# Seven half-products for eight in 24 of the 32 w_up tiles, with w_down's products between them

## The chip, the cores and the metric

The kernel runs on one NeuronCore of a Trainium2 chip, as one launch. The metric is device time in microseconds (us), the median of several runs; smaller is better. The engines are TensorE (PE in the profile; PEld is its weight load), VectorE (DVE), ScalarE (ACT), GpSimd (POOL) and SyncE (SP), which starts most DMAs. Each engine works through its own instructions in order and waits for others by semaphores.

## What is computed

A two-layer decoder trunk over 512 tokens of width 1024, in float32: two kinds of attention, gated and added, an output projection, then an MLP. The MLP is where the change lies:

```python
    x = x + mixed @ w_out
    h = rmsnorm(x, norm_mlp)
    return x + jnp.square(jax.nn.relu(h @ w_up)) @ w_down
```

`w_up` is 1024 x 4096, `w_down` 4096 x 1024. A final rmsnorm follows the second layer.

## The kernel before

Everything is kept transposed: features on the 128 partitions, the 512 tokens along the free axis. x is eight tiles of 128 x 512. A product with a weight matrix makes output tiles of 128 columns of the weight, each from eight K tiles.

Each float32 operand is split into two float32r parts, a high one (`h`, a rounding copy made on ACT) and a low one (`lo`, what is left, made by a subtraction on DVE or POOL). `gemm` (L202) makes three matmuls per K tile: high by high, high by low, low by high. So an output tile of w_up or w_down is 8 x 3 = 24 matmuls of 128 x 128 by 128 x 512.

Weights come in a fixed order, the list that `order` (L678) yields. `fetch` (L161) starts the next 512 KB load into a `raw` buffer on SP's queue; `convert` (L169) splits the oldest loaded one, `wh` by a cast on ACT (L182) and `wl` by a subtraction on DVE (L183), and fetches again; `weights` (L187) hands out the split parts. `gemm` calls `ahead` after its second K tile, so that the next weights are split while this product runs. There are two `raw`, two `wh` and two `wl` buffers.

A list scheduler puts the instructions of each engine in an order when the program is built, from the order of the source and its own costs; the order in the source is therefore not always the order on an engine. Buffers of one tag are a pool (`BUFS`, L150): an allocation waits until one of them is free.

The MLP of a layer (L902 to L945) goes in four chunks of 1024 columns of w_up. A chunk is eight up tiles, each 24 matmuls into one of PSUM's eight banks (`bank`, in turn), and then eight down tiles, each 24 matmuls over the chunk's eight activations, added to x on DVE (L939). The norm's factor per token, R, comes out of `rstd` (L256) while the first up tiles run; the input `u` is x times the gain only, and `act` (L906) applies R afterwards:

```python
            nc.vector.scalar_tensor_tensor(t, ps, 0.0, R, op0=OP.max, op1=OP.mult)   # L908
            nc.scalar.activation(h, t, AF.Square)                                    # L911
            nc.gpsimd.tensor_tensor(t, t, t, op=OP.mult)                             # L912
            nc.gpsimd.tensor_tensor(lo, t, h.bitcast(F32), op=OP.subtract)           # L913
```

The last chunk's down tiles of the second layer are `last` (L949), which works on 256 tokens at a time, so its matmuls have 256 columns, and ends with the final norm and the output. `sumsq` (L234) adds up squares on POOL (L249); `make_u` (L226) makes `u`.

Of the kernel before, what the change touches and what calls it, by code (L numbers as in the profile page):

```python
# [11 lines left out]
F32 = mybir.dt.float32  # L12
F32R = mybir.dt.float32r
# [4 lines left out]
L = 2  # L18
# [56 lines left out]
def col_blocks(w):  # L75
    """[K, M] -> [M/128, 128 (row in K tile), K/128, 128 (column)]"""
    k, m = w.shape
    return np.ascontiguousarray(w.reshape(k // 128, 128, m // 128, 128).transpose(2, 1, 0, 3))


def row_chunks(w):
    """[1024, M] -> [4, 128, 2, M]: two K tiles a chunk"""
    return np.ascontiguousarray(w.reshape(4, 2, 128, w.shape[1]).transpose(0, 2, 1, 3))


def layout(a):
    d = {}
    d["xT"] = np.ascontiguousarray(a["x"].reshape(T, D).T.reshape(KT, 128, T))
    wb, wva, wg2, wo, wout, wup, wdn, w1, small = ([] for _ in range(9))
    for l in range(L):  # L90
# [19 lines left out]
        wdn.append(np.stack([col_blocks(a["w_down"][l][c * 1024:(c + 1) * 1024]) for c in range(4)]))  # L110
# [14 lines left out]
    d["wout"], d["wup"], d["wdn"], d["w1"], d["small"] = st(wout), st(wup), st(wdn), st(w1), st(small)  # L125
# [15 lines left out]
class Body:  # L141
# [27 lines left out]
    def convert(self):  # L169
        """Splits the next loaded weights into two float32r parts, and starts a load in their place."""  # L170
# [16 lines left out]
    def weights(self, src, n=1024):  # L187
        """The parts of src, which is the next of the plan."""
# [35 lines left out]
    # ---- norms  # L224
# [9 lines left out]
    def sumsq(self, x, acc, last=False):  # L234
        """adds x * x to the list of tiles whose sum over tiles and partitions is wanted"""
# [51 lines left out]
    # ---- projections in token layout  # L287
# [30 lines left out]
    # ---- pairs of heads  # L318
# [37 lines left out]
    def q_pair(self, x, fox=False):  # L356
        """[q hi; q lo] of both heads, and with `fox` [q hi; 1; 1; 0 ...] of each."""
# [17 lines left out]
    # ---- causal attention of one head  # L375
# [73 lines left out]
    def out_half(self, O, o, e):  # L449
        """o[64e:64e+64] = O[:64] + O[64:]"""  # L450
# [124 lines left out]
    def cmp_probs(self, hk, q2):  # L575
        """Probabilities of the four heads of kv head hk over the compressed blocks, transposed."""
# [41 lines left out]
    # ---- a layer  # L618
# [16 lines left out]
    def forget(self, z):  # L635
        """cumulative log sigmoid, negated: CC rows 0-7 its upper part, rows 32-39 the rest"""
# [27 lines left out]
    def bank(self):  # L664
        """a bank of PSUM, any of the eight in turn"""
# [8 lines left out]
    def order(self, l):  # L674
        """The weights of a layer in the order of their use: [name, source, columns]"""
# [22 lines left out]
        for c in range(4):  # L698
            yield from ((flat(a["wup"][l, 8 * c + j]), 1024) for j in range(8))
            yield from ((flat(a["wdn"][l, c, m]), 1024) for m in range(8))  # L700

    def layer(self, l, u):
        nc, a = self.nc, self.a
        wb = a["wb"][l].rearrange("m p k c -> m p (k c)")
        # values of FoX and NSA, forget and branch gates: tokens on partitions
# [52 lines left out]
        # FoX  # L758
# [39 lines left out]
        # NSA  # L798
# [26 lines left out]
        def half(kind, m, w):  # L825
            """y_a or y_b, output tile m"""
# [39 lines left out]
        # gates of NSA, the mix, output projection  # L866
# [35 lines left out]
        # MLP  # L902
        R = None
        pend = []

# [10 lines left out]
        for c in range(4):  # L916
# [170 lines left out]
```

## Time and profile before

| | |
|---|---|
| median of 3 runs | 1568.53 us (1568.13 to 1568.83) |
| span of the profiled execution | 1567.0 us |
| MLP of the first layer, about | 430 to 780 us of the span |
| MLP of the second layer, about | 1205 us to the end |
| HBM read | 140.77 MB |

The span runs from the first to the last instruction of one profiled execution; the median is over other executions, without a profile, and is 1.5 us longer. In a row of a timeline stand the start, the duration, engine, line, operation, the tile written and the tiles read, their sizes, and in brackets how long the engine had been idle and what released it. In a row of groups stand the count, busy time, mean duration in ns, and idle time before. In a row of one tile or line: the shortest, median and longest duration in ns. In a row of windows: the length of the window, the busy time of PE, PEld, DVE, ACT and POOL with counts, the granted PE clock (1.00 is full), the busy share of the DMA engines and GB/s. A row of waits tells which engine and line waited for which, the total, how often, and the longest.

### The profile page before, as it was taken

How to read it: one execution, taken by the hardware profiler on the slowest of the kernel's cores; microseconds unless marked ns; L12 is line 12 of the kernel's file. 1: busy time of each engine (PE TensorE's matmuls, PEld its weight loads, DVE VectorE, ACT ScalarE, POOL GpSimd, SP SyncE). 2: the span in 40 equal slices, each digit the busy share in tenths (PEclk: the TensorE clock that was granted, in tenths of full speed). 3: DMA queues.
4: the chain of work that ended last, by engine and by line, in shares of the span. 5: the costliest groups of instructions: out<-in, count | busy, mean ns of one | idle time of the engine just before them, and what ended most of it. 6: DMA issues, size and time to landing. Idle time of an engine off the chain costs nothing.

```text
span 1567.0 us, 20175 instructions
## 1 busy us (share of the span) xinstructions
PE 1553.8 (99%) x7596; PEld 1282.8 (82%) x7596; DVE 885.4 (57%) x1804; ACT 627.3 (40%) x1135; POOL 258.5 (16%) x209
## 2 busy tenths in 40 slices
PE   9999999999999999999999999999999999999997
PEld 8867888888888888888887688888888888888887
DVE  5687988866443333333646689887564433333343
ACT  6444665543432222223443456555434312222243
POOL 4000000000241322304400000000002504132252
PEclk9999999999999999999999999999999999999999
DMA  6545422132222222222435543222322222232231
GB/s 238 169 133 156 118 81 81 61 108 97 98 94 95 94 101 101 95 95 101 177 115 166 160 132 95 68 68 68 120 96 94 95 94 95 99 103 95 95 121 54
DMA packets 56625, 169.42 MB, mean 108 GB/s; under 512 B 7344, under 2 KB 8112, under 8 KB 56528
## 3 DMA queue, kind: packets, MB, share of 16 engines
q1 hardware_dynamic: 53072, 161.84, 32.2%
q10 hardware_dynamic: 3456, 6.29, 1.2%
q8 instruction: 60, 0.98, 0.2%
q14 instruction: 37, 0.30, 0.1%
HBM read 140.77 MB, written 4.19 MB: 93 GB/s over the span
## 4 chain that ended last, share of the span: by engine, by line
PE 77%; issue 13%; POOL 6%; DVE 3%; ACT 1%; DMA 0%; POOLq 0%; DVEq 0%; SPq 0%; ACTq 0%
PE ps_mm L208 12%; PE ps_mm L209 11%; PE ps_mm L210 11%; PE ps_O L443 4%; PE ps_PT L417 3%; POOL tmp L912 3%; PE ps_S L208 3%; PE ps_S L210 3%; PE ps_S L209 3%; PE ps_PT L208 3%; POOL ol L913 3%; PE ps_PT L210 3%; PE ps_PT L209 3%; PE ps_O L210 3%; PE ps_O L209 2%
## 5 line engine op out<-in xcount | busy, mean ns | idle before, releaser
L182 ACT CAST wh<-raw 128x1024 fp32r<-128x1024 f32 (+2 forms) x235 | 243.3, 1036 | 612.4 <-PE ps_mm L209 155.9
L183 DVE TENSOR_TENSOR wl<-raw,wh 128x1024 fp32r<-128x1024 f32 (+2 forms) x235 | 287.1, 1222 | 53.6 <-ACT wh L182 45.1
L208 PE MATMUL ps_mm<-uh,wh 128*128 128x512 f32 x608 | 242.8, 399 | 0.0
L210 PE MATMUL ps_mm<-uh,wl 128*128 128x512 f32 x608 | 239.9, 395 | 0.0
L209 PE MATMUL ps_mm<-ul,wh 128*128 128x512 f32 x608 | 239.8, 394 | 0.0
L912 POOL TENSOR_TENSOR tmp<-tmp 128x512 f32<-128x512 f32 x64 | 97.5, 1524 | 440.5 <-ACT oh L911 440.5
L395 ACT ACTIVATE E<-E,mx 128x128 f32<-128x128 f32 x192 | 108.0, 563 | 81.6 <-DVE mx L394 74.5
L208 PEld LDWEIGHTS ps_mm<-uh,wh 128*128 128x128 f32 x608 | 114.3, 188 | 30.3 <-issue 10.6
L210 PEld LDWEIGHTS ps_mm<-uh,wl 128*128 128x128 f32 x608 | 114.3, 188 | 24.0 <-issue 0.8
L209 PEld LDWEIGHTS ps_mm<-ul,wh 128*128 128x128 f32 x608 | 114.6, 189 | 18.8
L209 PE MATMUL ps_mm<-ol,wh 128*128 128x512 f32 (+1 forms) x288 | 111.4, 387 | 0.6 <-POOL ol L913 0.6
L208 PE MATMUL ps_mm<-oh,wh 128*128 128x512 f32 (+1 forms) x288 | 111.7, 388 | 0.0
L210 PE MATMUL ps_mm<-oh,wl 128*128 128x512 f32 (+1 forms) x288 | 111.4, 387 | 0.0
L426 ACT CAST pth<-ps_PT 128x512 fp32r<-128x512 f32 x144 | 72.8, 512 | 94.9 <-PE ps_PT L417 94.7
L394 DVE CUSTOM_DVE_ANT_0 E<-ps_S,ct 128x128 f32<-128x128 f32 x192 | 92.3, 484 | 26.6 <-PE ps_S L391 25.2
L249 POOL TENSOR_TENSOR acc<-sq 128x512 f32<-128x512 f32 (+1 forms) x6 | 8.4, 1405 | 594.5 <-DVE wl L183 580.5
L427 DVE TENSOR_TENSOR ptl<-ps_PT,pth 128x512 fp32r<-128x512 f32 x144 | 85.1, 596 | 27.7 <-ACT pth L426 27.3
L417 PE MATMUL ps_PT<-ct,E 128*128 128x128 f32 x480 | 83.1, 274 | 1.4 <-DVE ptl L427 1.4
L913 POOL TENSOR_TENSOR ol<-tmp,oh 128x512 fp32r<-128x512 f32 x64 | 83.3, 1301 | 5.0
L417 PEld LDWEIGHTS ps_PT<-ct,E 128*128 128x128 f32 x480 | 60.1, 140 | 14.7 <-DVE ptl L427 4.2
L388 PE MATMUL ps_S<-kd,q 128*128 128x256 f32 x192 | 63.8, 338 | 0.0
L208 PEld LDWEIGHTS ps_mm<-oh,wh 128*128 128x128 f32 x288 | 54.2, 188 | 11.0 <-issue 1.5
(325 smaller groups left out, 3223.7 us busy)
## 6 DMA issues: line engine op xcount, KB each, us to landing
raw<-wb SPq DMA_DIRECT2D x64, 512.0 KB, 3.5
raw<-wup SPq DMA_DIRECT2D x64, 512.0 KB, 3.5
raw<-wdn SPq DMA_DIRECT2D x64, 512.0 KB, 3.4
kd<-hl SPq DMA_DIRECT2D x48, 256.0 KB, 4.7
w<-w SPq DMA_DIRECT2D x32, 256.0 KB, 5.9
q<-hl SPq DMA_DIRECT2D x64, 128.0 KB, 3.2
raw<-wo SPq DMA_DIRECT2D x16, 512.0 KB, 3.5
raw<-wout SPq DMA_DIRECT2D x16, 512.0 KB, 3.4
```

Source lines behind the costliest of these rows:

```text
L182: nc.scalar.copy(h[:, :n], raw[:, :n])
L183: nc.vector.tensor_tensor(lo[:, :n], raw[:, :n], h[:, :n].bitcast(F32), op=OP.subtract)
L208: mm(ps, h[:, c], xh, start=start and i == 0, stop=False)
L209: mm(ps, h[:, c], xl, start=False, stop=False)
L210: mm(ps, lo[:, c], xh, start=False, stop=stop and i == ks - 1)
L394: nc.vector.tensor_tensor_reduce(e, ps[:, :n], self.mask[:, T - n:], -1.0, BIG, OP.add, OP.min, mx)
L395: nc.scalar.activation(e, e, AF.Exp, bias=mx, scale=-1.0, accum_out=sm[:, i:i + 1])
L417: nc.tensor.transpose(ps[:, j * 128:(j + 1) * 128], E[i][:, b * 128:(b + 1) * 128], self.ident)
L426: nc.scalar.copy(h[:, o:o + n], ps[:, :n])
L427: nc.vector.tensor_sub(lo[:, o:o + n], ps[:, :n], h[:, o:o + n].bitcast(F32))
L912: nc.gpsimd.tensor_tensor(t, t, t, op=OP.mult)
L913: nc.gpsimd.tensor_tensor(lo, t, h.bitcast(F32), op=OP.subtract)
```

## The change

The first eight up tiles of a layer (`PLAIN`) stay as they were. The other 24 are made in twelve pairs by Strassen's scheme in Winograd's form. A pair's weights (1024 rows, 256 columns) are cut into four quarters A11, A12, A21, A22 of 512 rows by 128 columns, the normalised input into four quarters B of 512 rows by 256 tokens. Seven products of such quarters and of their sums and differences, each 4 K tiles x 3 matmuls of 128 x 128 by 128 x 256, give the four quarters of the two output tiles, where the plain way has eight such products.

`prepare` makes the seven input operands once per layer, split into high and low parts: it needs R applied first. Its steps are taken between the plain tiles, four a tile, and during the first six down blocks. `Strassen.load` fetches the raw weights of a pair (two loads of 512 KB) two pairs ahead, `Strassen.convert` makes the seven weight operands of the next pair (two sums on POOL, two on DVE, seven high parts on ACT, seven low parts on DVE) while `unit` makes the products of this one. The outputs come out of seven combinations on DVE and one copy on ACT, and `Strassen.act` applies relu, square and the split (three operations on ACT, one on POOL).

The down products of the first six groups of 512 rows of w_down (`wd2`) are made in 48 blocks of 4 x 3 matmuls, each added to x: six after the plain tiles, then four between the products of each pair (two in the eleventh pair, none in the twelfth). One 512 KB load holds the weights of two blocks; its raw buffer is the single one of the tag `crs`. The last 1024 rows stay as eight down tiles (or `last`).

In the built program the new steps of `prepare` stand on DVE among the evacuations of the plain tiles and the splits of their weights; after R, in the first layer, two evacuations, the first round of `prepare` with the third evacuation in it, then the split of the fifth plain tile's weights, and so on; the order is the same in the second layer.

Line numbers in the diff's new parts, where the text names them, are those of the changed kernel. Comments and docstrings that the diff only strikes out are left out here.

```diff
@@ layout
-        wdn.append(np.stack([col_blocks(a["w_down"][l][c * 1024:(c + 1) * 1024]) for c in range(4)]))
+        wdn.append(col_blocks(a["w_down"][l][3072:]))
+        b = a["w_down"][l][:3072].reshape(6, 4, 128, 4, 2, 128)
+        wd2.append(b.transpose(0, 3, 2, 4, 1, 5).reshape(6, 4, 128, 1024))
@@ fetch
-            src, n = self.plan.popleft()
-            raw = self.t(self.raws.popleft() if self.raws else "raw", [128, 1024], name="raw")
+            src, n, *tag = self.plan.popleft()
+            tag = tag[0] if tag else self.raws.popleft() if self.raws else "raw"
+            raw = self.t(tag, [128, 1024], name="raw")
@@ order
-        for c in range(4):
-            yield from ((flat(a["wup"][l, 8 * c + j]), 1024) for j in range(8))
-            yield from ((flat(a["wdn"][l, c, m]), 1024) for m in range(8))
+        yield from ((flat(a["wup"][l, j]), 1024) for j in range(self.PLAIN))
+        yield from ((a["wd2"][l, c, m], 1024, "crs") for c in range(6) for m in range(4))
+        yield from ((flat(a["wdn"][l, m]), 1024, *(("crs",) if m == 0 else ())) for m in range(8))
@@ the MLP, now mlp
+        def down(c, m, w):
+            ps = self.bank()
+            yield from self.gemm(ps, w, 4 * (m % 2), acts[4 * c:4 * c + 4], ks=4)
+            nc.vector.tensor_add(x[m], x[m], ps)
...
+        S = Strassen(self, l, x, gm)
+        D = downs()
+        g0 = self.PLAIN // 2
+        S.load(g0)
+        for j in range(self.PLAIN):
+            ps = self.bank()
+            w = self.weights(a["wup"][l, j].rearrange("p k c -> p (k c)"))
+            run(self.gemm(ps, w, 0, u))
...
+                R, _ = self.rstd(acc, (self.turn_tag(), self.turn_tag()))
+                prep = S.prepare(R)
...
+            act(ps)
+            for _ in range(4):
+                next(prep, None)
+        S.load(g0 + 1)
+        conv = S.convert(g0)
+        for i in range(6):
+            next(D)()
+            next(prep, None)
+            next(prep, None)
+            if i == 3:
+                run(prep)
+            if i > 3:
+                for _ in range(2):
+                    next(conv, None)
+        run(conv)
+        for g in range(g0, 16):
+            S.load(g + 2)
+            n = 4 if g < 14 else 2 if g == 14 else 0
+            S.unit(g, D, n, acts)
@@ new: class Strassen
+    def prepare(self, R):
...
+        for p in range(4):
+            q = []
+            for i in (p, p + 4):
+                t = b.t("t2", [128, T], name="bs")
+                V.scalar_tensor_tensor(t, self.x[i], self.gm[:, i:i + 1], R, op0=OP.mult, op1=OP.mult)
+                q.append(t)
+                yield
+            (b11, b12), (b21, b22) = ((t[:, :256], t[:, 256:]) for t in q)
+            t12, t34 = (b.t("t2", [128, 2, 256], name="ts") for _ in range(2))
+            V.tensor_tensor(t12[:, 0], b12, b11, op=OP.subtract)
+            V.tensor_tensor(t12[:, 1], b22, t12[:, 0], op=OP.subtract)
+            yield
+            V.tensor_tensor(t34[:, 0], b12, b22, op=OP.subtract)
+            V.tensor_tensor(t34[:, 1], b21, t12[:, 1], op=OP.subtract)
+            yield
+            A = nc.scalar
+            A.copy(t12h[:, :, p], t12)
+            A.copy(t34h[:, :, p], t34)
+            A.copy(h11[:, p], b11)
+            A.copy(h21[:, p], b21)
+            A.activation(h22[:, p], b22, AF.Copy, scale=-1.0)
+            f = lambda ap: ap.bitcast(F32)
+            V.tensor_tensor(t12l[:, :, p], t12, f(t12h[:, :, p]), op=OP.subtract)
+            yield
+            V.tensor_tensor(t3l[:, p], t34[:, 0], f(t34h[:, 0, p]), op=OP.subtract)
+            V.tensor_tensor(t4l[:, p], t34[:, 1], f(t34h[:, 1, p]), op=OP.subtract)
+            yield
+            V.tensor_tensor(l11[:, p], b11, f(h11[:, p]), op=OP.subtract)
+            V.tensor_tensor(l21[:, p], b21, f(h21[:, p]), op=OP.subtract)
+            yield
+            V.scalar_tensor_tensor(l22[:, p], b22, -1.0, f(h22[:, p]), op0=OP.mult, op1=OP.subtract)
+            yield
...
+    def convert(self, g):
...
+        G.tensor_tensor(s1, a21, a22, op=OP.add)
+        G.tensor_tensor(s3, a11, a21, op=OP.add)
+        ops = self.ops[g] = []
+        for i, src in enumerate((a11, s1, s2, a22, s3, a12, s4)):
+            if i == 2:
+                nc.vector.tensor_tensor(s2, s1, a11, op=OP.add)
+                nc.vector.tensor_tensor(s4, s2, a12, op=OP.add)
+            h = b.t("uh", [128, 512], F32R, name="sh")
+            lo = b.t("ul", [128, 512], F32R, name="sl")
+            nc.scalar.copy(h, src)
+            nc.vector.tensor_tensor(lo, src, h.bitcast(F32), op=OP.subtract)
+            ops.append((h, lo))
+            yield
...
+    def product(self, ps, g, i):
+        h, lo = self.ops[g][i]
+        xh, xl = self.xs[i]
+        mm = self.nc.tensor.matmul
+        for p in range(4):
+            c = slice(p * 128, (p + 1) * 128)
+            mm(ps, h[:, c], xh[:, p], start=p == 0, stop=False)
+            mm(ps, h[:, c], xl[:, p], start=False, stop=False)
+            mm(ps, lo[:, c], xh[:, p], start=False, stop=p == 3)
...
+    def unit(self, g, D, n, acts):
+        conv = self.convert(g + 1)
...
+        p5 = product(1)
+        next(conv, None)
+        between()
+        p6 = product(2)
+        sub(y[:, 1], y[:, 0], p6)
+        sub(c1[:, 256:], y[:, 1], p5)
+        next(conv, None)
+        p4 = product(3)
+        next(conv, None)
+        between()
+        p7 = product(4)
...
+    def act(self, c, pair, i):
+        h = b.t("oh", [128, T], F32R)
+        lo = b.t("ol", [128, T], F32R)
+        nc.scalar.activation(c, c, AF.Relu)
+        nc.scalar.activation(c, c, AF.Square)
+        nc.scalar.copy(h, c)
+        nc.gpsimd.tensor_tensor(lo, c, h.bitcast(F32), op=OP.subtract)
```

More of the change, by code (lines that the diff above doesn't have):

```diff
@@ L88, in layout @@
     d["xT"] = np.ascontiguousarray(a["x"].reshape(T, D).T.reshape(KT, 128, T))
-    wb, wva, wg2, wo, wout, wup, wdn, w1, small = ([] for _ in range(9))
+    wb, wva, wg2, wo, wout, wup, wdn, wd2, w1, small = ([] for _ in range(10))
     for l in range(L):
@@ L900, in layer, with mlp @@
             acc = self.sumsq(x[m], acc, m == 7)
+        return self.mlp(l, x, u, acc, gm)
+    PLAIN = 8
+    def mlp(self, l, x, u, acc, gm):
+        nc, a = self.nc, self.a
         R = None
         pend = []
+        acts = []
         def act(ps):
@@ new lines, in down, with downs @@
+        def down(c, m, w):
+            ps = self.bank()
+            yield from self.gemm(ps, w, 4 * (m % 2), acts[4 * c:4 * c + 4], ks=4)
+            nc.vector.tensor_add(x[m], x[m], ps)
+        def downs():
+            for c in range(6):
+                for m in range(8):
+                    if m % 2 == 0:
+                        w = self.weights(a["wd2"][l, c, m // 2])
+                    yield lambda: run(down(c, m, w))
+        S = Strassen(self, l, x, gm)
+        D = downs()
+        raws = [None] * 16
@@ new lines, in mlp @@
+        S.load(g0 + 1)
[14 more added lines that the diff above has]
+            S.unit(g, D, n, acts)
+        u_next = []
@@ new lines, in mlp @@
+        acts = acts[24:]
+        if l + 1 < L:
+            acc = []
+            self.load_small(l + 1)
+            for m in range(8):
+                ps = self.bank()
+                w = self.weights(a["wdn"][l, m].rearrange("p k c -> p (k c)"))
+                run(self.gemm(ps, w, 0, acts))
+                nc.vector.tensor_add(x[m], x[m], ps)
+                acc = self.sumsq(x[m], acc, m == 7)
+                u_next.append(self.make_u(x[m], self.gain[:, 16 * l + 16:16 * l + 24], m))
+                nc.scalar.dma_start(self.xs[m], x[m])
+        else:
+            self.last(x, acts, a["wdn"][l])
```

104 lines of the change are left out of this document (74 added, 30 removed).

## Prediction, made before the changed kernel ran

> **What bounds the kernel now.** I read the page first (busy shares), then the windows over the MLP, the waits, and the timelines of PE, DVE, POOL and ACT around the start of the first MLP.
>
> ```profile
> span 1567.0 us, 20175 instructions
> PE 1553.8 (99%) x7596; PEld 1282.8 (82%) x7596; DVE 885.4 (57%) x1804; ACT 627.3 (40%) x1135; POOL 258.5 (16%) x209
> 450.00:800.00 350.00, 350.00 (x1549) 289.89 (x1548) 134.43 (x141) 95.86 (x114) 102.53 (x80) 1.00 0.32 108
> DVE tmp L908 <- PE ps_S L210: 50.1, 15, 3.4
> ACT wh L182 <- PE ps_mm L209: 155.9, 65, 4.6
> ```
>
> The third line is the window 450 to 800 us of the first layer's MLP: PE is busy for all of it at clock 1.00, DVE for 134 of 350 us, ACT 96, POOL 103. Both helpers wait for PE (3.4 and 4.6 us at the longest), PE for nobody. So the MLP lasts as long as its matmuls, and a change there is worth the matmul time it removes, less every idle it brings to PE.
>
> ```profile
> 440.96 1.23 DVE L183 TENSOR_TENSOR wl<-raw,wh 128x1024 fp32r<-128x1024 f32 x1
> 445.27 0.69 DVE L908 SCALAR_TENSOR_TENSOR tmp<-ps_mm,R 128x512 f32<-128x512 f32 x1 [2.41 <-ACT R L284]
> 445.88 0.68 DVE L908 SCALAR_TENSOR_TENSOR tmp<-ps_S,R 128x512 f32<-128x512 f32 x1
> 452.92 0.69 DVE L908 SCALAR_TENSOR_TENSOR tmp<-ps_S,R 128x512 f32<-128x512 f32 x1 [2.65 <-PE ps_S L210]
> 459.19 1.23 DVE L183 TENSOR_TENSOR wl<-raw,wh 128x1024 fp32r<-128x1024 f32 x1
> 474.68 0.69 DVE L908 SCALAR_TENSOR_TENSOR tmp<-ps_S,R 128x512 f32<-128x512 f32 x1 [3.38 <-PE ps_S L210]
> 1542.82 0.28 PE L210 MATMUL ps_S<-oh,wva 128*128 128x256 f32 x1
> 1549.54 0.28 PE L209 MATMUL ps_O<-ol,wq 128*128 128x256 f32 x1
> ```
>
> L908 evacuates an up tile right behind its last matmul. Four tiles lie between 452.92 and 474.68: 5.44 us a tile of 24 matmuls, 0.2267 us each at 512 columns. The last two rows are the first and the last of 57 consecutive matmuls of 256 columns, in the kernel's last stage, with the same order of operands and a weight load for each: 6.72/56 = 0.120 us, a little more than half.
>
> **The change, term by term.** *Products.* A pair of up tiles was 2 x 5.44 = 10.88 us. It becomes seven products of 4 x 3 = 12 matmuls, 84 x 0.120 = 10.08 us: one eighth fewer columns, but 0.80 us a pair and not 1.36, because a half-width matmul costs more than half. Twelve pairs in two layers: 24 x 0.80 = **-19.2 us**. The down products keep their number (48 blocks of 12 matmuls for 24 of 24) and their weight bytes.
>
> By the Trainium skill, "TensorE: Matmul & The Clock Gate", section "Back-to-back issue gap", the warm gap is N/2.4 + 2.5 ns, 109 and 216 ns; by that estimate the pairs would save 24 x (48 x 0.2158 - 84 x 0.1092) = 28 us. The rows measure 120 and 227, so I go by them.
>
> *A pair in its steady run* (seven products and four down blocks, 10.08 + 10.88 = 20.96 us of PE).
>
> ```profile
> L535 DVE TENSOR_TENSOR x<-g x2: 424/425/426, 140.4 to 913.2; 128x256 f32<-128x256 f32 x2
> L231 DVE SCALAR_TENSOR_TENSOR ul<-x,gain,uh x32: 741/748/1847, 4.7 to 1204.1; 128x512 fp32r<-128x512 f32 x32
> L748 POOL TENSOR_TENSOR crs<-crs,R x4: 1295/1299/1410, 33.1 to 805.4; 128x512 f32<-128x512 f32 x4
> L912 POOL TENSOR_TENSOR tmp<-tmp x64: 1040/1523/2028, 446.8 to 1510.5; 128x512 f32<-128x512 f32 x64
> L911 ACT ACTIVATE oh<-tmp 128x512 fp32r<-128x512 f32 x64 | 40.4, 632 | 1.5 <-DVE tmp L908 1.5
> L182 ACT CAST wh<-raw 128x1024 fp32r<-128x1024 f32 x225 | 236.8, 1052 | 597.7 <-PE ps_mm L209 155.9 <-PE ps_PT L209 123.5 <-PE ps_S L209 121.0
> raw<-wup SPq DMA_DIRECT2D x64, 512.0 KB, 3.5
> ```
>
> DVE instructions that follow each other start 0.08 us before the one ahead is over (445.27 + 0.69 against 445.88), so one occupies 0.61 us at 512 elements, 1.15 at 1024, 0.34 at 256, and 0.67 for L231's kind. DVE per pair: 7 combinations of products at 0.34, 7 low parts and 2 sums of weight halves at 0.61, 4 additions to x at 0.61, 2 low parts of w_down weights at 1.15: 12.6 us. POOL: 2 sums and 2 low parts at 1.3, 5.2. Even one after the other that is 17.8, under 20.96. ACT: 13 operations of 512 at 0.55, 2 casts of 1024 at 0.97, one of 256 at 0.4: 9.5. DMA: four loads of 512 KB in 20.96 us, 100 GB/s against 108 now. All of that hides under PE: no charge, while the order holds (third rival).
>
> *The start of the MLP* is where I see the price. The halves of h must be normalised, combined and split before the first pair: `prepare`, four rounds, each with 2 scalings of 512, 4 combinations of 256, one low part of 512 and 5 of 256 on DVE, 5 copies on ACT. In the built program's order this stands on DVE between the L908s of the plain tiles and the low parts of their weights (L183), which PE needs. One round: 2 x 0.67 + 0.61 + 9 x 0.34 = 5.0 us. From R (445.27) to the low part of the third pair of w_down blocks, DVE has: 8 L908 4.9, four rounds 20.0, 7 of L183 8.05, 2 additions to x 1.2, 5 low parts and 2 sums for the first pair of tiles 4.3: **38.5 us**. PE wants that last L183 after the eighth plain tile (474.45, that is 474.68 less the 0.23 from a product's end to L908) and four down blocks of 2.72, plus two matmuls: 485.8. DVE alone would be there at 483.8. But POOL squares and splits the eight plain tiles in the same time, and these two queues exclude each other:
>
> ```profile
> 447.89 1.30 POOL L913 TENSOR_TENSOR ol<-tmp,oh 128x512 fp32r<-128x512 f32 x1
> 448.27 2.00 DVE L183 TENSOR_TENSOR wl<-raw,wh 128x1024 fp32r<-128x1024 f32 x1 [0.17 <-ACT wh L182]
> 449.15 2.02 POOL L912 TENSOR_TENSOR tmp<-tmp 128x512 f32<-128x512 f32 x1
> 398.62 0.75 DVE L231 SCALAR_TENSOR_TENSOR ul<-x,gain,uh 128x512 fp32r<-128x512 f32 x1
> 398.72 1.79 POOL L249 TENSOR_TENSOR acc<-sq 128x512 f32<-128x512 f32 x1 [290.20 <-DVE wl L183]
> 1539.59 2.19 DVE L1001 TENSOR_TENSOR y<-x,R 128x256 f32<-128x256 f32 x3 [0.43 <-ACT R L284]
> 1539.64 2.74 POOL L1001 TENSOR_TENSOR y<-x,R 128x256 f32<-128x256 f32 x3 [8.23 <-ACT R L284]
> ```
>
> L183 issued at 448.27 ends at 450.27, 1.1 us after POOL's L913 (449.19); POOL's L912, issued at 449.15, ends 0.9 after L183. Same for L231 and L249: 398.72 + 1.79 is 1.14 after L231's end. With three equal instructions on each side (L1001) the six take 2.79 us, about the 3 x 0.34 + 3 x 0.6 of one after the other: strict turns, nobody passes twice. All three DVE forms read two operands from SBUF, as every instruction of `prepare` does; L908 and the additions read PSUM and one from SBUF.
>
> POOL's share: eight tiles at 2.3 (L912 1.04, L913 1.29) and two weight sums at 1.3, 21.0 us. So the third pair's L183 ends between 483.8 (POOL costs nothing) and 445.27 + 38.5 + 21.0 = 504.8 (all in turn); if the 6.1 us of DVE work that reads PSUM lie over POOL's, 498.7. PE's delay there: 0 to 19.0, with turns 12.9 to 19.0. Not in that sum: DVE waits for ACT's copies in each round, and the single buffer that holds a w_down pair's raw weights, which makes each load wait for the L183 before it (3.5 + 1.05 + 1.15 = 5.7 us from one L183 to the next, PE uses a pair in 5.44). I take 18 us per layer, close to the upper end for these. The first piece shows already at the fifth plain tile: its L183 has 3 L908, one round and itself ahead, 8.0 us of DVE and 6.9 of POOL, 460.2, and PE wants it at 453.1: 7 us idle. On SP two loads for the second pair of tiles stand ahead of the second w_down load; they wait for the L183s of the last plain tiles, which DVE has done by then, so they add no wait, only traffic. Late next is everything behind PE by the same 18 us, with nothing to win it back. The second layer's program has the same order. **+36 us.**
>
> *The end.*
>
> ```profile
> PE ps_mm L209 <- POOL ol L913: 0.6, 1, 0.6
> ```
>
> The last two activations now come 2.88 us of products apart, so this wait may go: -0.6 at best, 0 at worst; I take -0.6.
>
> **Sum:** 1567.0 - 19.2 + 36 - 0.6 = 1583.2 us of span; the runs' median lies 1.5 us above the span: **1585 us**, slower by 1%. Own range 1575 to 1593 (12.9 to 22 us a layer).
>
> **Rivals.** *The queues pass each other* (the side of faster): DVE gets through and POOL waits, or the order leaves gaps I don't see. Then PE idles 0.1 to 0.7 us at the fifth tile and the gain stands: 1568.5 - 19.2 + 1.4 - 0.6 = 1550. For it: the DVE sum alone fits (483.8 before 485.8). Against: all three pairs of rows above show turns. It decides from 9.6 us of idle per layer downwards, where the gain is eaten up. *Half the overlap*: PE's first 7 us of idle push the later plain tiles, and POOL's work on them, out of DVE's crowded stretch; with half of POOL's 21.0 the third pair comes at 494.3, 8.5 us late: 1566. *Short in the steady run*: each w_down pair's L183 stands behind the addition of the block before; it has two products, 2.88 us, and two matmuls 0.45, and needs 0.25 + 0.61 + 1.15 plus one turn of POOL, 1.3: 3.31 of 3.33. If every second of the 42 w_down pairs of both layers' steady runs misses by half a turn, 0.65: +14, 1599. *A slower clock behind each stall*:
>
> ```profile
> L1039 PE MATMUL ps_PT<-ones 128*128 128x128 f32 x20 | 4.6, 430 | 1.1 <-DVE ones L1035 1.1
> L657 PE MATMUL ps_S<-ones,f 128*8 128x128 f32 x24 | 3.6, 272 | 0.0
> ```
>
> PE's first 20 matmuls after its start take 430 ns where the same size takes 272 later. If three stalls a layer each restart PE like that, 4.6 x (1 - 272/430) = 1.7 us each: +10, 1595. Against: no idle of that length stands in this trace, and the windows give clock 1.00. The Trainium skill, same page, section "What's actually happening", speaks for it: after an idle window of about 3.4 us PE falls to half clock for about as long. By that estimate it is again 1.7 us a stall; no run here shows it yet.
>
> **How the numbers follow.** Forecast 0.52, queues pass 0.15, half the overlap 0.10, slower clock 0.13, short in the steady run 0.10. The range 1558 to 1604 leaves out the passing queues and the tops of the last two. A difference under 0.2%, 3 us, can't be told from none here. Faster: 0.15 and half of 0.10, and a little of the forecast's low end, 0.21; same 0.05; slower 0.74.
>
> **What would show it.** In the changed profile: PE idle of about 7 us near 453 us with a DVE low part (wl) as its releaser, more of it up to about 505, the same 770 us later; DVE over 90% busy from 446 to 500; `prepare`'s 256-element instructions well over 0.42 us where POOL works; matmuls of 256 columns 0.120 us apart in the pairs; no PE wait from the third pair on. It is wrong if PE runs without a gap from 447 to 495, if the pairs' matmuls come slower than 0.120, or if PE waits inside the steady run.

## The result and the profile after

| | before | after |
|---|---|---|
| median of 4 runs each, side by side | 1568.33 us (1567.40 to 1568.83) | 1587.12 us (1586.96 to 1589.12) |
| span of the profiled execution | 1567.0 us, mean clock 0.998 | 1587.3 us, mean clock 0.989 |

Ratio 1.0124, 95% interval 1.0111 to 1.0136: the change makes the kernel 1.2% slower. The head of the page after:

```profile
span 1587.3 us, 22775 instructions
PE 1549.3 (98%) x8460; PEld 1313.4 (83%) x8460; DVE 1104.4 (70%) x2236; ACT 765.6 (48%) x1415; POOL 259.0 (16%) x209
```

PE has only 4.5 us less busy time than before (1553.8), though the matmuls that were saved are worth more. Busy time hides a slow clock, so the next view is the windows over the first layer's MLP (start and end, length, then the busy time of PE, PEld, DVE, ACT and POOL with their instructions, the granted clock, DMA):

```profile
450.00:800.00 350.00, 338.25 (x1936) 297.64 (x1935) 241.57 (x348) 161.79 (x249) 104.52 (x81) 0.98 0.32 104
453.00:461.00 8.00, 2.23 (x9) 1.56 (x8) 8.00 (x12) 2.96 (x5) 2.96 (x3) 0.74 0.00 0
490.00:500.00 10.00, 6.72 (x21) 5.10 (x22) 9.96 (x11) 3.75 (x7) 6.70 (x5) 0.83 0.17 52
600.00:760.00 160.00, 160.00 (x1010) 145.34 (x1009) 100.71 (x159) 78.22 (x120) 35.31 (x28) 1.00 0.28 89
```

The whole difference sits at the start: in the steady run (last row) PE is busy for 160 of 160 us at full clock. At 453 to 461 PE has work for 2.23 of 8 us, DVE is busy for all 8, and the clock is down to 0.74. PE's waits (engine, tile and line that waits, what it waits for: us in total, times, the longest; `ps_mm` and `ps_PT` are banks of PSUM, given out in turn in both layers, and of the six waits for `wl` three are in each layer) and PE's timeline around the first of them:

```profile
PE ps_mm L214 <- DVE wl L187: 10.6, 3, 5.8
PE ps_PT L214 <- DVE wl L187: 10.6, 3, 5.8
PE ps_mm L213 <- POOL ol L1260: 1.3, 1, 1.3
```

```profile
453.76 0.39 PE L212 MATMUL ps_PT<-uh,wh 128*128 128x512 f32 x1
453.99 0.39 PE L213 MATMUL ps_PT<-ul,wh 128*128 128x512 f32 x1
460.15 0.80 PE L214 MATMUL ps_PT<-uh,wl 128*128 128x512 f32 x1 [5.77 <-DVE wl L187]
460.74 0.63 PE L212 MATMUL ps_PT<-uh,wh 128*128 128x512 f32 x1
461.17 0.63 PE L213 MATMUL ps_PT<-ul,wh 128*128 128x512 f32 x1
...
463.30 0.57 PE L212 MATMUL ps_PT<-uh,wh 128*128 128x512 f32 x1
463.71 0.40 PE L213 MATMUL ps_PT<-ul,wh 128*128 128x512 f32 x1
463.95 0.39 PE L214 MATMUL ps_PT<-uh,wl 128*128 128x512 f32 x1
```

PE stands 5.8 us for the low part of the weights (L187 is the old L183), and then starts matmuls 0.43 us apart, not 0.227, until 463.7. Adding up, from R to the first product, what each start lies later than the spacing allows gives 17.9 us in the first layer and 18.0 in the second, in two kinds: 12.3 us of waits in each, and 5.5 and 5.6 us of slow matmuls behind them.

The pairs' steady run repeats every seven products and four blocks:

```profile
599.77 0.28 PE L1196 MATMUL ps_O<-t,sh 128*128 128x256 f32 x1
620.81 0.28 PE L1196 MATMUL ps_PT<-t,sh 128*128 128x256 f32 x1
```

21.04 us, where two old tiles and their share of down tiles took 4 x 5.44 = 21.76. A pair saves 0.72 us, 24 pairs 17.3. Spans: 1567.0 - 17.3 + 35.9 + 0.7 (the wait on L1260 near the end, 1.4 us in PE's spacing where 0.8 was before) + 1.1 (R of the first layer comes at 445.76, before at 444.65; in the runs below that were made from the changed kernel it came at 443.9 to 446.6, so this part may be chance) = 1587.4, against 1587.3.

### The profile page after: what moved, and what is told of

Read it like the earlier page. It is cut to its first block, busy times and chain, and to the rows that moved or that the text cites. A ratio compares the mean times of both kernels' runs of the same rounds, so it can differ in the third digit from the quotient of the medians.

```text
span 1587.3 us, 22775 instructions
## 1 busy us (share of the span) xinstructions
PE 1549.3 (98%) x8460; PEld 1313.4 (83%) x8460; DVE 1104.4 (70%) x2236; ACT 765.6 (48%) x1415; POOL 259.0 (16%) x209
## 4 chain that ended last, share of the span: by engine, by line
PE 88%; DVE 9%; issue 1%; DMA 1%; ACT 1%; SPq 0%; POOL 0%; DVEq 0%; POOLq 0%; ACTq 0%
PE ps_mm L212 11%; PE ps_mm L214 11%; PE ps_mm L213 11%; PE ps_O L447 4%; PE ps_PT L421 3%; PE ps_PT L214 3%; PE ps_PT L212 3%; PE ps_PT L213 3%; PE ps_S L212 2%; PE ps_S L213 2%; PE ps_S L214 2%; PE ps_O L212 2%; PE ps_O L213 2%; PE ps_O L214 2%; PE ps_S L392 2%; PE ps_S L395 2%
## 5 line engine op out<-in xcount | busy, mean ns | idle before, releaser
L186 ACT CAST wh<-raw 128x1024 fp32r<-128x1024 f32 (+2 forms) x187 | 192.5, 1030 | 250.3 <-PE ps_mm L213 61.8
L187 DVE TENSOR_TENSOR wl<-raw,wh 128x1024 fp32r<-128x1024 f32 (+2 forms) x187 | 227.3, 1215 | 52.4 <-ACT wh L186 51.6
L214 PE MATMUL ps_mm<-uh,wl 128*128 128x512 f32 x512 | 203.2, 397 | 5.8 <-DVE wl L187 5.8
L212 PE MATMUL ps_mm<-uh,wh 128*128 128x512 f32 x512 | 205.6, 402 | 0.0
L213 PE MATMUL ps_mm<-ul,wh 128*128 128x512 f32 x512 | 202.7, 396 | 0.0
L212 PEld LDWEIGHTS ps_mm<-uh,wh 128*128 128x128 f32 x512 | 96.6, 189 | 26.8 <-issue 10.6
L1260 POOL TENSOR_TENSOR ol<-c,oh 128x512 fp32r<-128x512 f32 x48 | 62.7, 1306 | 312.6 <-ACT oh L1259 312.6
L213 PEld LDWEIGHTS ps_mm<-ul,wh 128*128 128x128 f32 x512 | 96.7, 189 | 15.3
L1185 ACT CAST sh<-raw 128x512 fp32r<-128x512 f32 x72 | 44.6, 620 | 111.3 <-PE ps_PT L1197 29.8
L1186 DVE TENSOR_TENSOR sl<-s,sh 128x512 fp32r<-128x512 f32 x96 | 78.2, 815 | 26.0 <-ACT sh L1185 26.0
L1185 ACT CAST sh<-s 128x512 fp32r<-128x512 f32 x96 | 59.6, 621 | 71.5 <-PE ps_mm L1197 16.9
```

Source lines behind the costliest of these rows:

```text
L186: nc.scalar.copy(h[:, :n], raw[:, :n])
L187: nc.vector.tensor_tensor(lo[:, :n], raw[:, :n], h[:, :n].bitcast(F32), op=OP.subtract)
L212: mm(ps, h[:, c], xh, start=start and i == 0, stop=False)
L213: mm(ps, h[:, c], xl, start=False, stop=False)
L214: mm(ps, lo[:, c], xh, start=False, stop=stop and i == ks - 1)
L1185: nc.scalar.copy(h, src)
```

## The experiments

"Delay" is, from here on, PE's from R to the first product, per layer, summed from the spacing of its matmuls as above: waits and slow matmuls together. All times stand beside runs of the kernel before on the same chip.

### Take DVE's part away, or POOL's

The first leaves out `prepare`'s DVE instructions; in the second the plain tiles lose POOL's:

```diff
-                V.scalar_tensor_tensor(t, self.x[i], self.gm[:, i:i + 1], R, op0=OP.mult, op1=OP.mult)
...
-            A.copy(t12h[:, :, p], t12)
+            A.activation(t12h[:, :, p], half(b1), AF.Copy, scale=1e-3)
...
+        self.xs = [(h, h) for h in xh]
```

> The changed kernel without the DVE instructions of prepare: ACT copies the plain x instead (scaled by 0.001), and the high part stands in for the low part, so the products are not the right ones; number and order of all else stay. Theory (the price of the change is the 20 us of prepare on DVE in each layer, in line with POOL): the DVE work from R to the third w_down pair falls from 38.5 to 18.5 us, with all of POOL's 21.0 in line 39.5, under the 40.5 us that PE needs; PE idles under 2 us a layer there, and the whole gain of the pairs shows: 1587.1 - 36 = 1551, between 1548 and 1556. Rival A (the w_down pairs' single raw buffer sets the stalls): they stay at 3 us or more a layer and the time is above 1560. Rival B (the pairs themselves save less than 19 us, or the steady run stalls): PE has no gap, and yet the time is above 1557.

```diff
-            nc.gpsimd.tensor_tensor(t, t, t, op=OP.mult)
-            nc.gpsimd.tensor_tensor(lo, t, h.bitcast(F32), op=OP.subtract)
-            acts.append((h, lo))
+            acts.append((h, h))
```

> The changed kernel without POOL's two instructions on each plain tile (the square and the low part; the high part stands in for the low part, so the result lacks those low parts); prepare and all of DVE's and ACT's work stay. Theory (DVE and POOL exclude each other): of POOL's 21.0 us 18.4 go, the third pair's low part comes 0 to 3 us late instead of 18; PE stands 0 to 4 us a layer, time 1551 to 1560. Rival A (DVE's own queue, its waits for ACT and the single raw buffer set the stall, POOL is beside it): it stays at 12 us or more a layer, 1575 or above. Rival B (half and half, as turns were not strict): 6 to 12 us a layer, 1563 to 1575.

Without `prepare`'s DVE work: 1558.15 us, ratio 0.9938 (0.9923 to 0.9953). Without POOL's work on the plain tiles: 1556.38 us, ratio 0.9925 (0.9911 to 0.994). The windows from 446 to 512 us, first of the changed kernel, then of these two:

```profile
446.00:512.00 66.00, 54.25 (x220) 43.02 (x219) 61.72 (x82) 26.97 (x46) 33.72 (x20) 0.90 0.25 75
```

```profile
446.00:512.00 66.00, 64.41 (x321) 54.03 (x320) 43.86 (x51) 25.57 (x37) 30.46 (x21) 1.00 0.35 112
```

```profile
446.00:512.00 66.00, 64.85 (x324) 54.73 (x323) 59.23 (x102) 34.14 (x57) 11.93 (x7) 1.00 0.36 112
```

The third row is the one to read: DVE does all its work, 102 instructions in place of 82, at 59 us busy, and the delay is 1.7 to 1.8 us in place of 18. From R to the low part of the third w_down pair DVE does the same 72 instructions in both kernels. Counted from start to start, they last 16.5 us longer in the changed kernel than they do alone, and 2.4 us longer in this run; DVE idles for under 2 us in either. So it is the instructions themselves that are held up, not DVE waiting for a buffer. The length of DVE's queue alone is no stall, and POOL's work alone is none (second row, 1.8 to 2.4 us). Only the two together are. What is left are mostly low parts of w_down pairs. The first run missed its range by 2 us, half on rival B's side: a pair saves 0.72, not 0.80, and PE lost 2.8 us more than before near the end (waits of 1.8 and 0.3 us and slow matmuls). 1567.0 - 17.3 + 2.4 + 1.8 + 2.8 is 1556.7, its span.

### The same work, given out evenly

```diff
-            for _ in range(4):
+            for _ in range(2):
                 next(prep, None)
...
-            next(prep, None)
-            next(prep, None)
+            for _ in range(4):
+                next(prep, None)
```

> The changed kernel with prepare's steps given out more slowly over the plain tiles (two behind a tile, not four) and faster over the six blocks behind them (four behind a block, not two); all the work is the same. Theory (the sum of DVE's and POOL's work from R to the third pair sets it): the first idle, 5.9 us in front of the fifth plain tile, goes or falls under 2 us, and comes back in front of the third pair and the first product; the sum of idle and slow matmuls stays within 14 to 20 us a layer, time 1582 to 1590. Rival (the stall is that of a burst ahead of the plain tiles' low parts, and DVE has room later): it falls below 10 us a layer, time below 1571.

1583.65 us, ratio 1.0099 (1.0082 to 1.0116). The delay is 17.1 and 15.6 us: the 5.8 us wait is 1.7 now, and eight others of 0.6 to 3.8 us follow it, the longest for the `wh` of a w_down pair. The sum decides, as long as the window stays the same. One place of this run shows something else (PE's timeline):

```profile
499.11 0.39 PE L213 MATMUL ps_PT<-ol,wh 128*128 128x512 f32 x1
501.39 0.50 PE L214 MATMUL ps_PT<-oh,wl 128*128 128x512 f32 x1 [1.90 <-DVE wl L187]
501.73 0.40 PE L212 MATMUL ps_PT<-oh,wh 128*128 128x512 f32 x1
501.97 0.46 PE L213 MATMUL ps_PT<-ol,wh 128*128 128x512 f32 x1
502.22 0.63 PE L214 MATMUL ps_PT<-oh,wl 128*128 128x512 f32 x1
...
505.62 0.39 PE L213 MATMUL ps_O<-ol,wh 128*128 128x512 f32 x1
```

After a wait of 1.9 us PE starts again at full rate, and falls to half rate 0.8 us later, for 3.40 us.

### Idle and the clock, in the kernel before

```diff
-        nc.vector.tensor_tensor(lo[:, :n], raw[:, :n], h[:, :n].bitcast(F32), op=OP.subtract)
+        self.made += 1
+        for _ in range(self.again.get(self.made, 1)):
+            nc.vector.tensor_tensor(lo[:, :n], raw[:, :n], h[:, :n].bitcast(F32), op=OP.subtract)
```

> The kernel before, with the low part of single w_up tiles made 5, 6, 7, 8 and 10 times over in the first layer's MLP, far apart, and 7, 7, 7 and 6, 6, 6 times on tiles in a row in the second's, so that PE idles about 1.1, 2.2, 3.4, 4.5 and 6.8 us. The result is the same. What is asked: after which idle PE runs at half rate (0.43 us between matmuls of 512 columns, not 0.227), and for how long. Theory from the changed kernel's trace, where this came after idles of 5.9, 3.2 and 2.0 us: from 2 us upward, for 7 to 8 matmuls, 1.5 us each. Rival, the Trainium skill, TensorE: Matmul & The Clock Gate, section What's actually happening (an idle window of about 3.4 us): only behind the 3.4, 4.5 and 6.8 us idles, and for about as long, 1.6 us lost; nothing behind those of 1.1 and 2.2 us. Rival C: the loss grows with the idle.

One run, 1642.77 us. The idles came out larger and more alike than meant (at each place one of 0.7 to 0.9 us, one matmul, and then the one in the table). What each cost beyond the idle itself:

| idle, us | 2.4 | 4.5 | 4.4 | 4.4 | 4.4 | 8.9 | 4.9 | 6.6 | 3.4 |
|---|---|---|---|---|---|---|---|---|---|
| slow matmuls, us lost | 1.4 | 2.5 | 1.9 | 2.7 | 2.5 | 2.4 | 1.5 | 1.6 | 2.7 |
| full rate again at, us | 535.76 | 566.41 | 638.09 | 668.75 | 754.10 | 1354.77 | 1371.96 | 1457.37 | 1477.77 |

The loss doesn't grow with the idle (rival C falls: 8.9 us cost 2.4, 3.4 us cost 2.7), and the idle of 2.4 had it too, as the theory said; its "7 to 8 matmuls, 1.5 us" is only about the smallest case. Four single idles of 0.6 to 1.1 us had no slow matmul behind them. What orders the table is its last line: 566.41 - 535.76 = 30.65 = 9 x 3.41, 638.09 - 566.41 = 71.68 = 21 x 3.41, and over the whole length 942.01 = 276 x 3.413. Full rate comes back on a fixed grid of 3.413 us, whenever the idle was. The previous experiment shows the other edge: half rate from 502.22 to 505.62, one step, after a step (498.81 to 502.22) in which PE stood for 2.05 us by its spacing; 1.78 us within one step (464.68 to 468.09, same run) had no such effect. In the changed kernel three waits a layer cross that line. The Trainium skill, "TensorE: Matmul & The Clock Gate", section "What's actually happening", has this as a free-running window of 3413 ns over PE's activity; the trace agrees with the grid, while of the idle window that it names as the cause (about 3.4 us) 2.05 us of idle were enough here.

### Less work in the window, or a longer window

Three runs: the plain tiles' square made by ACT; ten blocks in front of the first product, not six; both.

```diff
-            nc.scalar.activation(h, t, AF.Square)
-            nc.gpsimd.tensor_tensor(t, t, t, op=OP.mult)
+            nc.scalar.activation(t, t, AF.Square)
+            nc.scalar.copy(h, t)
```

> The changed kernel with the plain tiles' square made in place by ACT, which then copies the high part, as the pairs have it; POOL keeps only the low part. The result is the same. POOL's work in the crowded stretch falls by 8 x 1.04 = 8.3 us, from 21.0 to 12.7; ACT's grows by 8 x 0.55 = 4.4. Theory (DVE's and POOL's times add up): the 18 us of delay a layer, idle and slow matmuls together, become 7 to 11, time 1566 to 1573. Rival A (POOL's square runs beside DVE, only the low part hurts): 16 us or more, 1583 or above. Rival B (ACT, a link between DVE's steps, becomes the bound): longer than the changed kernel, with PE or DVE waiting for ACT.

```diff
-        for i in range(6):
+        for i in range(10):
...
-            n = 4 if g < 14 else 2 if g == 14 else 0
+            n = 2 if g < 6 else 4 if g < 14 else 2 if g == 14 else 0
```

> The changed kernel with ten w_down blocks in front of the first product, not six (the first two pairs then have two blocks between their products, not four), and prepare's steps two behind a plain tile and two behind a block. The result is the same. PE's window grows by 4 x 2.72 = 10.9 us, DVE's work in it by 4 x 0.61 + 2 x 1.15 = 4.7, of which 2.4 reads PSUM. Theory (it is the sum of work against the window): the delay of 18 us a layer becomes 9.5 to 12, and with fewer slow matmuls time 1566 to 1575. Rival A (the first two pairs are too short of cover with two blocks, DVE 10.2 + POOL 5.2 = 15.4 of 15.5 us): 2 us or more a layer come back inside them, waits for sl or sh, 1571 to 1580. Rival B (a burst, not a sum): the delay goes altogether, 1555 or below.

> Both: ten blocks first with prepare's steps two at a time, and the plain tiles' square on ACT. The result is the same. Theory: 18 - 8.3 - 6.2 to 8.6 leaves 1 to 4 us a layer, under what sets off slow matmuls if it comes in pieces; 1587.1 - 2 x 15.5 = 1556, between 1552 and 1562, faster than the kernel before. Rival A (the first two pairs fall short): up to 4 us more, 1560 to 1567. Rival B (the two don't add up, since each takes away the same stall): 1562 to 1570.

| | median, us | ratio (95%) | delay, layers 1 and 2, us |
|---|---|---|---|
| square on ACT | 1573.62 | 1.0035 (1.0021 to 1.0048) | 10.6, 10.6 |
| ten blocks first | 1572.86 | 1.0028 (1.0017 to 1.0039) | 9.5, 11.5 |
| both | 1563.32 | 0.9964 (0.9952 to 0.9977) | 6.3, 4.5 |

In the two with ten blocks `prepare`'s last round reads x[3] after the fourth block's addition to it, so a part of the products is made from that x. The delays of the first two are those expected, and the sum of work against a window holds: 18 - 8.3 = 9.7 (measured 10.6), 18 - 6.1 to 8.6 = 9.4 to 11.9. Together they should have left 1 to 4 us and left 4.5 to 6.3: 2 us in front of the last pair of blocks, where the low part of its weights stands behind `prepare`'s last round on DVE, 0.4 at each earlier pair, and 0.5 and 0.6 among the plain tiles. No wait for `sl` or `sh` appeared, so rival A of the second and third run falls.

These runs also narrow down when half rate sets in. In the run with the square on ACT two waits, each under 1.5 us, are followed by it (PE's timeline):

```profile
486.71 0.50 PE L212 MATMUL ps_mm<-oh,wh 128*128 128x512 f32 x1 [1.23 <-ACT wh L186]
487.05 0.40 PE L213 MATMUL ps_mm<-ol,wh 128*128 128x512 f32 x1
487.97 0.61 PE L214 MATMUL ps_mm<-oh,wl 128*128 128x512 f32 x1 [0.53 <-DVE wl L187]
488.38 0.63 PE L212 MATMUL ps_mm<-oh,wh 128*128 128x512 f32 x1
...
491.72 0.39 PE L214 MATMUL ps_mm<-oh,wl 128*128 128x512 f32 x1
```

By the spacing PE stood for 1.39 and 0.70 us, 2.09 together within one step (full rate is back at 491.72, so the step before the slow one is 484.89 to 488.31). And in the two runs with ten blocks the wait in front of the last pair is nearly the same in both layers, 1.94 and 1.96 us in one run, 1.97 and 1.93 in the other; behind 1.96 and 1.97 about 1.6 us of slow matmuls follow, behind 1.94 and 1.93 none. That is most of the 2 us by which the delays of the two layers differ in these rows.

### The rest of it: one raw buffer, and an order that the builder chose

```diff
-        yield from ((a["wd2"][l, c, m], 1024, "crs") for c in range(6) for m in range(4))
+        yield from ((a["wd2"][l, c, m], 1024, "raw" if (c, m) in ((0, 1), (0, 3)) else "crs")
+                    for c in range(6) for m in range(4))
```

> As e7, with three more moves: prepare's steps go four behind each of the first blocks (the last round then reads x before the blocks add to it, so the result is the reference's), the first pair's conversion starts at the seventh block one step at a time, and the second and fourth w_down pairs load into the w_up buffers that are free then (the second pair of tiles loads behind them). Theory: what was left in e7, about 5 us a layer (0.4 at each w_down pair from the single raw buffer, 2.0 in front of the last one from prepare's last round on DVE), falls to 0 to 2 us a layer; time 1553 to 1559. Rival A (the work only moves: the low parts of the early pairs stand behind four steps each): 4 to 6 us a layer stay, 1560 to 1566.

> As e8, but all w_down pairs load into their one buffer again. The result is the same. Theory (one buffer makes 5.7 to 5.9 us from one low part to the next, PE uses a pair in 5.44): waits of 0.3 to 0.5 us at each of the pairs two to five, 1.2 to 2 us a layer, the time 2.5 to 4 us above e8. Rival (DVE is what makes a pair late, the buffer has time): within 1 us of e8.

With all moves of the first expectation, of which the excerpt shows the buffer, 1565.38 us, ratio 0.9981 (0.9971 to 0.999), and with the one buffer 1572.97 us, 1.003 (1.0019 to 1.0041). The buffer matters, 7.6 us where 2.5 to 4 were expected: the delay is 7.1 us a layer with two and 10.2 with one, as the longest wait grows from 2.2 to 3.1 us (slow matmuls follow it in both) and three waits of 0.3 to 1.1 us come at the pairs behind it. But with its last round mended the kernel is slower than it was (1565.38 against 1563.32). The windows of the mended kernel:

```profile
446.00:486.00 40.00, 36.59 (x156) 28.60 (x155) 39.79 (x61) 24.29 (x44) 16.08 (x9) 1.00 0.22 67
486.00:512.00 26.00, 25.40 (x114) 21.23 (x115) 20.71 (x28) 7.92 (x12) 4.35 (x3) 0.93 0.45 142
```

DVE is full up to 486 us (39.79 of 40) and has 5 us free behind it: the list scheduler that orders each engine when the program is built drew all four rounds in front of the first block's addition to x (their last instruction starts at 486.47, that addition at 487.40), though the source has steps behind the blocks. Where x[3] was read late, in the run with both, the last round's first instruction starts at 488.95, right behind the addition that it needed (488.23). So the next two kernels hold rounds back with a dependency that is harmless; the order of the blocks changes with it, and what that alone does was not tried:

```diff
+            gm = self.gm
+            if p > 1:
+                gm = b.t("gate", [128, 8])
+                V.scalar_tensor_tensor(gm, self.x[0 if p == 2 else 4][:, :8], 0.0, self.gm, op0=OP.mult, op1=OP.add)
```

> As e8 (ten blocks first, square on ACT, two pairs loaded into free w_up buffers), with the blocks of a w_down part in the order 0, 1, 4, 5, 2, 3, 6, 7 and with prepare's third and fourth round held back: their gains come from a small DVE instruction that reads x behind the first and the third block (0 times x, plus the gain), so that the built order can't draw them ahead between the plain tiles. The result is the same. Theory (the delay is work due in a window, and e8 had all four rounds in front of the first block, behind which three low parts came 0.5 to 2.2 us late): DVE's rounds three and four fall into the 27 us of the ten blocks, where POOL rests; PE's delay falls from 4.8 to 1 to 2.5 us a layer, time 1557 to 1562. Rival (the two rounds then make the late pairs' low parts late by as much): 1563 to 1568.

> As e10, with the rounds held back to the fifth and the seventh plain tile's high part and to x behind the first block. The result is the same. Theory: one round for each 11 us, 5.0 of a round, 1.2 of L922, 2.3 of low parts and 2.6 of POOL, 11.1 in all: no low part is more than 0.5 us late, 0 to 2 us a layer, time 1555 to 1560. Rival as for e10: 1563 to 1568.

1553.03 us, ratio **0.9902** (0.9886 to 0.9919), and 1553.43 us, 0.9904 (0.989 to 0.9919): both kernels are beaten, the one before by 1.0% and the changed one by 2.2% (from the two ratios), and the times are 2 to 4 us below what was expected. For the first the expectation set out from a delay of 4.8 us, the waits alone; with the slow matmuls it was 7.1. The same windows, of the first:

```profile
446.00:486.00 40.00, 39.57 (x175) 32.41 (x174) 34.03 (x55) 23.37 (x39) 12.50 (x8) 1.00 0.30 92
486.00:512.00 26.00, 26.00 (x139) 22.48 (x138) 25.91 (x41) 11.96 (x21) 9.38 (x6) 1.00 0.37 122
```

DVE rests for 6 us of the first 40 and is full in the second stretch, where no low part is late: PE's delay is 0.7 us, one wait of 0.59 by its spacing.

### The same with the square on POOL

The excerpt is against the kernel with two rounds held:

```diff
-            nc.scalar.activation(t, t, AF.Square)
-            nc.scalar.copy(h, t)
+            nc.scalar.activation(h, t, AF.Square)
+            nc.gpsimd.tensor_tensor(t, t, t, op=OP.mult)
```

> As e10, but the plain tiles' square is POOL's again. The result is the same. From R to the eighth plain tile (29.2 us) DVE has 4.9 of L922, 10.0 of prepare's two rounds and 7 low parts, 8.1, and POOL 18.7. Theory (their times add up, save for the 4.9 that read PSUM): 36.8 us of work against 29.2 and what slack the low parts have, 3.5 us; PE's delay is 3 to 7 us a layer, time 1558 to 1567. Rival (holding the rounds back is enough, POOL finds its turns between them): under 1.5 us a layer, 1552 to 1556.

1559.73 us, ratio 0.9943 (0.993 to 0.9957); delay 3.7 us in each layer, all of it among the plain tiles (waits of 1.65, 0.53 and 1.18 us), none behind 468 us. Among these kernels holding the rounds back, with the order of blocks that goes with it, is worth 12.4 us (1565.38 to 1553.03), and moving the square 6.7 (1559.73 to 1553.03).

## Why the prediction was right, point by point

*The sum.* -19.2 + 36 - 0.6 was forecast, 1585; it came out as -17.3 + 35.9 + 0.7 with 1.1 for an earlier stage, 1587.1.

*The pairs.* 256 columns took 0.120 us, as in the row that was quoted. The term is 0.08 us a pair too large, because the first matmuls of 512 columns behind those of 256 stand a little further apart (0.233 and 0.236 us, where it is 0.227 later): four blocks and seven products take 21.04, not 20.96 us.

*The steady run* is hidden. PE has no gap in the 160 us shown; the rival that put 14 us there had nothing.

*The stall at the start* was 18 us a layer and 17.9 and 18.0 were measured. The mechanism was the forecast one, DVE and POOL shutting each other out, but "strict turns, nobody passes twice" holds only in places. POOL's timeline in the changed kernel (the start, then the duration; L925 is the old L912):

```profile
447.89 1.34 POOL L925 TENSOR_TENSOR tmp<-tmp 128x512 f32<-128x512 f32 x1 [19.07 <-ACT oh L924]
449.31 1.63 POOL L926 TENSOR_TENSOR ol<-tmp,oh 128x512 fp32r<-128x512 f32 x1
...
461.44 4.89 POOL L925 TENSOR_TENSOR tmp<-tmp 128x512 f32<-128x512 f32 x1 [3.77 <-ACT oh L924]
...
476.45 3.42 POOL L925 TENSOR_TENSOR tmp<-tmp 128x512 f32<-128x512 f32 x1 [5.24 <-ACT oh L924]
```

```profile
449.71 1.52 DVE L1133 TENSOR_TENSOR ts<-bs 128x256 f32<-128x256 f32 x1
451.14 1.26 DVE L1136 TENSOR_TENSOR ts<-bs 128x256 f32<-128x256 f32 x1
...
461.94 0.41 DVE L1133 TENSOR_TENSOR ts<-bs 128x256 f32<-128x256 f32 x1
462.27 0.42 DVE L1136 TENSOR_TENSOR ts<-bs 128x256 f32<-128x256 f32 x1
```

At 449 to 453 they take turns, and a 256-element DVE instruction lasts 1.3 to 1.5 us, not 0.42. At 461.4 DVE goes through at full speed, and the same POOL instruction takes 4.9 us. So the turns are not strict. The forecast's sum can be redone from the trace, up to the low part of the third pair:

```profile
446.39 0.69 DVE L921 SCALAR_TENSOR_TENSOR tmp<-ps_mm,R 128x512 f32<-128x512 f32 x1 [2.41 <-ACT R L288]
501.96 1.21 DVE L187 TENSOR_TENSOR wl<-raw,wh 128x1024 fp32r<-128x1024 f32 x1
503.23 0.50 PE L214 MATMUL ps_PT<-oh,wl 128*128 128x512 f32 x1 [1.87 <-DVE wl L187]
```

From the first L921 to the end of this L187 are 56.8 us. Of these 38.5 are the forecast instructions at the lengths that they have alone, 16.5 is what they were stretched by, and 1.8 is idle, nearly all of it (1.75) for a tile that PE delivered late. The stretching lies within the forecast's 14.9 to 21.0 for POOL, at its lower end, though POOL made two more weight sums in this time than were counted, those of the second pair of tiles (497.16 and 499.59). Less the 40.5 us that PE needs, this makes 16.3 us, and PE's delay when it restarts at 503.23 is 16.2. The low part ends at 503.17, which is 502.05 if R is set to the time that it had before; forecast were 498.7 to 504.8.

What is missing to 18 are 1.7 us of slow matmuls behind this last wait, the term that had been set aside as a rival. Its price was right, 1.7 us a stall forecast and 5.5 a layer measured for three, 1.8 a stall (in part by luck: the two rows that it came from differ in the size of the weights, 128*128 and 128*8). But the time didn't go up by all of it: the slow matmuls behind the first two waits come before PE meets the same low part of the third pair, so they mostly make its last wait shorter (argued from the trace; no run takes the slow clock out). So the mechanism was right, and that the size is right to 0.1 us is luck: 18 was taken, near the upper end, for DVE's waits for ACT's copies and for the single raw buffer, and in this stretch DVE idled for neither. The 1.7 us that this was too much are about the 1.7 that the slow clock added. The single raw buffer has a price once DVE has less to do: a second one took 3.1 us off the delay of each layer where it was tried, with ten blocks first and the square on ACT.

*The fifth tile* was forecast to idle 7 us; it idled 5.8, released by the low part named, in both layers.

*The end.* -0.6 was the wrong sign. The wait on the last low part, now L1260, grew by 0.7 us. In the code that low part now stands behind three ACT operations on the tile (L1257 to L1259) where one stood before; whether these are the 0.7 us was not tried.

*Rivals.* "The queues pass each other" describes 461 to 465 and 476 to 479 us, where DVE goes through, and is wrong for the whole, since 16.5 us of stretching are left. "Half the overlap" put the third pair 8.5 us late; it was 16.2. "A slower clock" had its mechanism and price right and its sum too large, as above. That neither queue alone makes the stall was settled by taking out either side: DVE's work alone costs 1.7 to 1.8 us a layer, POOL's alone 1.8 to 2.4.

## What to carry to other kernels

Work that is hidden in the mean (DVE 70% busy here) can still stand in front of one small instruction that PE needs; compare, for each stretch, what is due on DVE and POOL together, where DVE's instructions read two operands from SBUF, with PE's time there. Before a large one-off piece of work is cut or moved to other engines, look where the builder put it, and hold it back with a dependency: that took 12 of the 34 us between the changed kernel (1.2% slower) and the best one (1.0% faster); the rest came from ten blocks first, the square on ACT and a second raw buffer. Count the slow clock wherever PE's idle within one step of 3.4 us adds up to about 2 us, in one stall or in two: it cost 1.4 to 2.7 us apiece here, whatever the stall's length.

## What was not expected of the hardware

POOL can be held out by DVE: a 128x512 product that takes 1.04 us alone took 4.89 us (461.44) while DVE issued two-operand SBUF instructions without a gap, though 12 us before the two had alternated. The Trainium skill, "SBUF — State Buffer", section "Who interferes with whom", has it that a DVE instruction with two SBUF inputs contends with a GpSimd instruction that reads SBUF, and that issue order decides who blocks. Both stretches agree with the contention (1.3 to 1.5 us for 0.42, 4.89 for 1.04); they show besides that who comes next is not settled by taking turns. Why the two differ was not found.

Half rate is set by a 3.413 us grid and not by the stall: nine recoveries in one run lie on it within 0.2 us, and 2.05 us of idle inside one step of it, or 1.39 and 0.70 together, halved the rate for the whole next step, where 1.78 us did not. Between them it turned on hundredths: 1.96 and 1.97 us did, 1.93 and 1.94 did not. Where each of these lies in its step may decide as well; that was not separated.
